# Order tables, a DRAM stop for attention outputs and one work list for a two-layer encoder's token sublayer

## The chip, the core and the metric

The kernel runs on one core of a Trainium2 chip. The core has five engines that run side by side and wait for each other through semaphores: TensorE (PE; its weight loads, PEld, overlap its matmuls), VectorE (DVE), ScalarE (ACT), GpSimd (POOL) and SyncE (SP). Data lies in DRAM, in SBUF (128 partitions) and in PSUM, which PE writes. DMAs are issued from SP's queue and from POOL's and share 16 DMA engines. The metric is the device time of one execution in microseconds; shorter is better.

## What is computed

A two-layer bidirectional encoder on one sequence of 512 tokens, width 1024, in float32. Cut to what matters:

```python
for i in range(DEPTH):                                   # DEPTH = 2
    proj = x @ w_in[i]                                   # 1024 -> 6656 columns
    q_na, k_na, v_na, q_r, k_r, v_r, g_r, gate_a, gate_b = jnp.split(proj, IN_SPLITS, axis=-1)
    ya = neighbourhood_attention(q_na, k_na, v_na, na_rpb[i])            # 8 heads of 64
    yb = bidirectional_retention(q_r, k_r, v_r, g_r, ...)                # 4 heads, 128 | 256
    merged = jax.nn.sigmoid(gate_a) * (ya @ w_branch_a[i]) + jax.nn.sigmoid(gate_b) * (yb @ w_branch_b[i])
    y = merged @ w_out[i]
    x = layer_norm(DEEPNORM_ALPHA * x + y, ln1_g[i], ln1_b[i])
    ffn = conv_glu_ffn(x, w_up[i], conv_w[i], conv_b[i], w_down[i])
    ple = jax.nn.sigmoid(x @ w_ple_gate[i]) * (p[i] @ w_ple_proj[i])
    x = layer_norm(DEEPNORM_ALPHA * x + ffn + ple, ln2_g[i], ln2_b[i])
```

## The kernel before

**Products.** Every operand of a matmul is split into two parts, `hi` (the value rounded to the matmul's input format) and `lo` (the rest), by a copy on ACT and a subtraction on DVE (`split`, lines 207 and 208). A product is three matmuls, hi by hi, hi by lo and lo by hi (`mm3`, lines 537 to 539). Weights come from DRAM as `raw` tiles of 128x1024 by SP's queue and are split on chip; of some tiles (`sent`) ACT makes both parts and POOL's queue adds the weight into `lo` by an accumulating DMA (line 495).

**Blocks.** The two value/retention-gate blocks (0 and 1) and the two gate blocks (2 and 3) of the input projection, the branch b product (B) and others are multiplied as a two by two block scheme with seven products instead of eight, `a, c, t1, t2, d, t3, t4`. Their operands are sums of quarters of weights and of activations. A sum of weights is made either by an accumulating DMA on POOL's queue (line 433) or, where a table (`ON_CHIP`, `BB_CHIP`) says so, by an addition on DVE (line 474). The sums of activations come from `quad_sums` (DVE at lines 916 to 931, parts at 909 and 912). A finished quarter of a block's result goes to an `emit`: gates pass through a sigmoid on ACT and are stored to DRAM (`gscr`), value blocks are split and kept.

**Space.** SBUF holds 30 `unit` tiles of 4 KB per partition (`N_UNIT`); split activations, intermediate results, loaded gates and some weights all take one and give it back after its last reader. A DMA into a unit waits until the earlier owner's readers are done, and everything behind it on the same queue waits too.

**Order.** In the token sublayer a head of the list, `VG[l]`, and then the list `FILL[l]` of each layer say which product comes next: `3t2` is product t2 of block 3, `nq1` and `nk1` are attention query and key projections, `q0` and `k0` those of retention, `vn` the attention values, `b` a quarter of branch a (`ba`: two token tiles by 512 columns), `Ba` to `Bt4` branch b's products, `P` one token tile of the output projection. Between the entries stand steps of the retention heads (`ret_head`, from the slots in `RET_AT` with offsets 0, 2, 3, 5) and the attention heads (`na_head`, from `NA_AT` with offsets 0, 2, 5). From the end of `VG` to the end of the sublayer the work is put in its final order by a scheduler from the order in which the code issues it; elsewhere the code's order is kept.

**The end of the sublayer.** `ya` are the attention outputs; turned and split they lie in four units `yat` (one per pair of heads) until branch a reads them. `ba` loads the four gate tiles `sa` of a token tile each and multiplies branch a into them (line 1282). `branch_b` is a generator: at its products it also loads the second gate (`M`, line 1306), makes the split quarters of `Y`, the retention output, and their sums (`yw`, `yq`), and after each product but the first it transposes (`turn`, line 1267, tile `tr`) what the product before it finished; behind the last product it transposes the last pairs. The turned result `mt` is the operand of the output projection (`proj_ln`, tile `gn`).

`early_x` (lines 1247 and 1252) multiplies and adds the normalisation's parameters into the residual `R` at the start of layer 1, at the slots of `PX_AT`. `PG[l]` is the order of the block behind the token sublayer (the per-layer embedding's gate together with the first up-projection tiles, `up`).

Of the kernel before, what the change touches and what calls it, by code (L numbers as in the profile page):

```python
# [14 lines left out]
P = 128  # L15
# [17 lines left out]
SENT = (('k0', 'nk2', 'q0', 'q2', 'q3', 'q1'), ('nq1', 'q3', 'nq3', 'k0'))  # L33
# [4 lines left out]
FILL = (('nk0', 'nq3', '3t2', '3d', 'vn', 'nq2', '3t3', 'nk2', '2c', '3t4', '2t1', '0a', '2d', '2t2',  # L38
# [7 lines left out]
RET_AT = ((36, 37, 38, 40), (38, 40, 38, 41))  # L46
NA_AT = ((8, 10, 13, 14, 15, 20, 21, 24), (8, 8, 9, 11, 14, 18, 19, 24))
ORD = ('vector', 'scalar', 'tensor', 'gpsimd', 'sync')
RESIDENT = {(l, c) for l in range(DEPTH) for c in (67, 68, 69, 70, 71)}
TURN_LAG = 1  # L50
OUT_PREP = ((0, 1, 2, 1), (0, 1, 1, 1))
# [3 lines left out]
VG = (('p0', 'p1', '3a', '3c', 'nq1', 'nk1', '2a', 'nq0', 'nk3', '3t1'),  # L55
      ('3a', '3c', '2a', 'nk2', '3t1', 'nq0', 'nq2'))

XN_AT = (0, 6)
M_AT = (1, 1)
TABLES_AT = (0, 8)  # L60
REST_AT = (1, 2, 5, 8, 11, 16)
SUM_AT = (-2, -1)
PLE_AT = (45, 22)
HOOK = (1, 1)
PX_AT = (8, 15, 15, 18, 19, 22, 39, 42, 42, 42)
GN_ACT = ((0, 1, 2, 3), (3,))
BSENT = (('4d', '1d'), ('4d',))
# [3 lines left out]
PG = (('a', 'c', 't1', 'up', 'up', 't2', 'Ua', 'Ut1', 'd', 't3', 'Ut2', 'Ud', 't4', 'Ut3', 'Uc', 'Ut4'),  # L71
 ('a', 'c', 't1', 'up', 'up', 't2', 'Ua', 'Ut1', 'd', 't3', 'Ut2', 'Ud', 't4', 'Ut3', 'Uc', 'Ut4'))
# [4 lines left out]
BB_CHIP = ('t2', 't2')  # L77
# [8 lines left out]
 ('D0a', 'D0c', 'D2c', 'U0c', 'u12', 'u13', 'u14', 'u2', 'u3', 'u5', 'u6', 'u9'))  # L86
# [26 lines left out]
ON_CHIP = (('t2 t3', 't2', '', ''), ('', '', 't1 t3', 't2 t3'))  # L113
BB_HELD = (('c', 'd', 't2', 't4', 't1'), ('c', 't2', 't4'))
BB_EARLY = ('a', 'd')
RC_ACT = ((0, 5), (4, 7))


def _ap(t, off, dims):
# [2125 lines left out]
```

## Time and profile before

| | us |
|---|---|
| three timed runs | 1665.73, 1665.70, 1664.40 (median 1665.7) |
| the profiled execution | 1665.84 |
| its span, first to last instruction | 1664.1 |
| DMA moved | 326.79 MB, mean 196 GB/s |
| busy: PE, DVE, ACT, POOL | 1642.6, 1350.8, 1049.6, 226.7 |

In rows of the profile a line number is that of the kernel; `out<-in` are the program's names without their numbers; `x` counts instructions. A busy PE is modelled: a matmul's row of 0.39 us begins 0.23 us after the row before it where nothing waits. In the timeline a bracket behind a row says how long the engine was idle before it and who ended that. "u", "v" and "w" are accumulators of the block products, "gt" of a projection by columns, "gn" of one by tokens.

The page's slices of the span (40 slices of 41.6 us, busy tenths) show PE at nine everywhere but in the last:

```profile
PE   9999999999999999999999999999999999999997
DVE  5857878878787988978988766789888889889788
ACT  6787875665367757447586887753644676564563
POOL 1101111111211210111100011100202211101112
```

### The profile page before, as it was taken

To read this page: it belongs to the slowest core of one execution; us is meant where nothing else is said; L and a number is where in the kernel's file an instruction comes from. 1 tells how busy PE (TensorE), PEld (TensorE's weight loads), DVE (VectorE), ACT (ScalarE), POOL (GpSimd) and SP (SyncE) were. 2 spreads that over 40 slices of the span, in tenths; PEclk is the share of its full clock that TensorE was granted. 3 is DMA by queue.
4 is the path that set the end of the run, shared out by engine and by line. 5 is a ranking of instruction groups with operands and counts; after the bars stand their busy time and mean duration, and the time that the engine had idled before them with its cause. 6 is when DMAs were issued, how large, how long until landed. Compare 5 with 4: busy or idle time off the path is not lost.

```text
span 1664.1 us, 23407 instructions
## 1 busy us (share of the span) xinstructions
PE 1642.6 (99%) x8679; PEld 1407.9 (85%) x8679; DVE 1350.8 (81%) x2063; ACT 1049.6 (63%) x1586; POOL 226.7 (14%) x277
## 2 busy tenths in 40 slices
PE   9999999999999999999999999999999999999997
PEld 7888888987889899889888888888878898988896
DVE  5857878878787988978988766789888889889788
ACT  6787875665367757447586887753644676564563
POOL 1101111111211210111100011100202211101112
PEclk9999999999999999999999999999999999999999
DMA  9859865566789877479656579533758897875693
GB/s 329 237 154 215 239 143 132 177 210 161 210 228 246 209 228 228 138 206 226 201 170 199 165 177 249 118 102 114 208 183 256 220 270 178 253 203 176 180 239 76
DMA packets 95442, 326.79 MB, mean 196 GB/s; under 512 B 10976, under 2 KB 11488, under 8 KB 95328
## 3 DMA queue, kind: packets, MB, share of 16 engines
q0 software_dynamic: 33984, 121.65, 36.3%
q1 hardware_dynamic: 61200, 203.39, 34.6%
q8 instruction: 68, 1.11, 0.3%
q14 instruction: 46, 0.38, 0.1%
q10 hardware_dynamic: 144, 0.26, 0.0%
HBM read 300.09 MB, written 26.21 MB: 196 GB/s over the span
## 4 chain that ended last, share of the span: by engine, by line
PE 87%; DVE 6%; issue 2%; DMA 2%; ACT 2%; POOL 0%; DVEq 0%; POOLq 0%; ACTq 0%
PE u L537 7%; PE u L539 7%; PE u L538 7%; PE gt L537 6%; PE u L138 6%; PE gt L539 6%; PE gt L538 6%; PE v L537 4%; PE v L539 4%; PE v L538 4%; PE gt L138 4%; PE v L138 4%; PE gn L537 3%; PE gn L538 3%; PE gn L539 3%
## 5 line engine op out<-in xcount | busy, mean ns | idle before, releaser
L208 DVE TENSOR_TENSOR lo<-rawa,hi 128x1024 fp32r<-128x1024 f32 (+1 forms) x150 | 178.6, 1201 | 58.6 <-ACT hi L207 57.9
L207 ACT CAST hi<-rawa 128x1024 fp32r<-128x1024 f32 (+1 forms) x150 | 153.4, 1034 | 102.0 <-DMA rawa<-in_wpack 30.3
L208 DVE TENSOR_TENSOR lo<-raw,hi 128x1024 fp32r<-128x1024 f32 x109 | 132.4, 1222 | 38.6 <-ACT hi L207 38.4
L433 POOL DMA_DIRECT2D rawa<-in_wpack x84 | 75.1, 894 | 556.9 <-DVE lo L208 427.1
L207 ACT CAST hi<-raw 128x1024 fp32r<-128x1024 f32 x109 | 113.4, 1049 | 58.2 <-DMA raw<-in_wpack 14.1
L537 PE MATMUL gt<-x1t,hi 128*128 128x512 f32 x256 | 100.2, 391 | 1.8 <-DVE ca L1568 1.8
L538 PE MATMUL gt<-x1t,hi 128*128 128x512 f32 x256 | 99.8, 390 | 0.0
L539 PE MATMUL gt<-x1t,lo 128*128 128x512 f32 x256 | 99.3, 389 | 0.0
L537 PE MATMUL gt<-xt,hi 128*128 128x512 f32 x224 | 87.7, 392 | 0.0
L539 PE MATMUL gt<-xt,lo 128*128 128x512 f32 x224 | 87.3, 390 | 0.0
L538 PE MATMUL gt<-xt,hi 128*128 128x512 f32 x224 | 87.3, 390 | 0.0
L495 POOL DMA_DIRECT2D lo<-in_wpack x34 | 30.3, 890 | 382.0 <-ACT lo L494 264.5
L138 DVE TENSOR_TENSOR lo<-rawa,hi 128x1024 fp32r<-128x1024 f32 x38 | 45.7, 1222 | 17.6 <-ACT hi L138 17.6
L537 PEld LDWEIGHTS gt<-x1t,hi 128*128 128x128 f32 x256 | 48.1, 188 | 12.9 <-issue 2.6
L539 PEld LDWEIGHTS gt<-x1t,lo 128*128 128x128 f32 x256 | 48.1, 188 | 10.1
L538 PEld LDWEIGHTS gt<-x1t,hi 128*128 128x128 f32 x256 | 48.1, 188 | 9.4
L207 ACT CAST hi<-rawt 128x1024 fp32r<-128x1024 f32 (+1 forms) x38 | 38.7, 1027 | 23.8 <-DVE rawt L474 14.3
L208 DVE TENSOR_TENSOR lo<-rawt,hi 128x1024 fp32r<-128x1024 f32 (+1 forms) x38 | 45.0, 1196 | 7.2 <-ACT hi L207 3.9
L138 ACT CAST hi<-rawa 128x1024 fp32r<-128x1024 f32 (+1 forms) x42 | 42.5, 1028 | 12.8 <-DMA rawa<-in_wpack 5.2
L537 PE MATMUL gn<-hi,mt 128*128 128x512 f32 x128 | 50.2, 395 | 0.0
L537 PE MATMUL u<-hi,s 128*128 128x512 f32 x128 | 50.0, 392 | 0.0
L538 PE MATMUL u<-lo,s 128*128 128x512 f32 x128 | 49.9, 390 | 0.0
(523 smaller groups left out, 5551.2 us busy)
## 6 DMA issues: line engine op xcount, KB each, us to landing
raw<-in_wpack SPq DMA_DIRECT2D x173, 512.0 KB, 5.2
rawa<-in_wpack POOLq DMA_DIRECT2D x108, 512.0 KB, 6.4
rawa<-in_wpack SPq DMA_DIRECT2D x46, 512.0 KB, 5.5
rawt<-in_wpack SPq DMA_DIRECT2D x46, 512.0 KB, 6.0
lo<-in_wpack POOLq DMA_DIRECT2D x44, 512.0 KB, 7.7
s<-s_scr POOLq DMA_DIRECT2D x32, 512.0 KB, 8.9
rawd<-in_wpack SPq DMA_DIRECT2D x30, 512.0 KB, 6.3
rawt<-in_wpack POOLq DMA_DIRECT2D x26, 512.0 KB, 8.2
```

The source lines that it names most:

```text
L138: r = f(*a, **k)
L207: nc.scalar.copy(hi, src)
L208: nc.vector.tensor_sub(lo, src, _f(hi))
L433: nc.gpsimd.dma_start(it.raw[:, :w], wpack[l, c][:, o:o + w], accum_op=ALU.add)
L495: nc.gpsimd.dma_start(lo[:, :w], wpack[l, c][:, o:o + w], accum_op=ALU.add)
L537: nc.tensor.matmul(ps, lh, rh, start=start, stop=False, skip_group_check=more)
L538: nc.tensor.matmul(ps, lh, rl, start=False, stop=False, skip_group_check=more)
L539: nc.tensor.matmul(ps, ll, rh, start=False, stop=stop, skip_group_check=more)
```

## The change

**Attention outputs wait in DRAM.** Of the four `yat` units of a layer, three (`Y_KEPT`) are stored to a new DRAM tensor `yscr` by SP's queue when they are made, and are loaded again by POOL's queue at the list entry `Y`.

**Branch b is split into list entries.** What `branch_b` did around its products has entries of its own in `FILL`: `Q` makes the next split quarter or sum (seven of them: a, c, t1, t2, d, t3, t4), `A` loads the next quarter of the first gate, `M` of the second, `X` loads the residual, `T` does two turns. These entries take no slot of their own.

**Gates by quarter.** `sa` and `M` were four tiles each of one token tile by 1024 columns; now they are four of two token tiles by 512, loaded one at a time, and a tile is given back after its second turn or use. The bytes are the same.

**The transposes of a retention head** come in two steps, one per pair of token tiles, with offsets of their own; retention and attention heads get offsets per head (`RET_OFF`, `NA_OFF`).

**New numbers** in most of the order tables: `FILL`, `VG`, the slots, which weights are `sent`, held or added on chip. By engine, counting rows of the built programs: PE 8692 and 8692; DVE 2065 and 2068, among them additions `rawt<-rawt,rawd` 20 and 26, scalings of `yb` 12 and 8; ACT scalings of `yb` 20 and 24, table loads 39 and 37; POOL accumulating loads `rawt<-in_wpack` 26 and 20, `yat<-y_scr` 0 and 6; SP stores `y_scr<-yat` 0 and 6.

The core of the diff:

```diff
-         '1d', 'q0', '1t2', 'q1', '0c', 'q2', '1t3', 'q3', '1t4', 'b', 'b', 'b', 'b', 'Ba', 'Bc',
-         'Bt1', 'Bd', 'Bt2', 'Bt3', 'Bt4'),
-        ('nk0', 'nq1', '3d', '3t2', 'nk1', '2c', '3t3', '3t4', 'vn', '2t1', '2d', '2t2', 'nk3', '0a',
...
-         'k1', 'k2', '1t3', '1d', '0c', 'q0', '1t4', 'q1', 'k3', 'q3', 'b', 'b', 'b', 'b', 'Ba',
-         'Bc', 'Bt1', 'Bd', 'Bt2', 'Bt3', 'P', 'Bt4', 'P'))
...
+         'k3', 'k1', '1d', 'q0', '1t2', 'q2', '1c', 'Y', '1t3', 'q3', '1t4', 'A', 'A', 'A', 'A', 'b',
+         'M', 'b', 'b', 'Q', 'Ba', 'Q', 'X', 'b', 'Q', 'Bc', 'Q', 'Bt1', 'Q', 'M', 'Q', 'Q', 'Bt2',
+         'Bd', 'M', 'Bt3', 'M', 'Bt4', 'T', 'T', 'T', 'P', 'T'),
...
+         'Y', 'k0', '0t4', '1t2', 'k2', '1t3', 'A', '0c', 'k1', 'q1', '1t4', 'k3', 'A', 'A', 'b',
+         'M', 'b', 'A', 'b', 'Q', 'Ba', 'b', 'Q', 'Q', 'Bt1', 'Bc', 'M', 'Q', 'M', 'Q', 'Q', 'M',
+         'Q', 'Bd', 'Bt2', 'X', 'Bt3', 'T', 'T', 'Bt4', 'T', 'P', 'T'))
...
+Y_KEPT = ((0, 1, 2), (0, 1, 3))
...
-PX_AT = (8, 15, 15, 18, 19, 22, 39, 42, 42, 42)
+PX_AT = (8, 14, 17, 18, 20, 24, 39, 42, 42, 42)
...
-BB_CHIP = ('t2', 't2')
+BB_CHIP = ('t1 t3', 't2')
...
-ON_CHIP = (('t2 t3', 't2', '', ''), ('', '', 't1 t3', 't2 t3'))
+ON_CHIP = (('t2 t3', 't1 t2 t3', '', 't3'), ('', 't3', 't2 t3', ''))
...
+                    if m in Y_KEPT[l]:
+                        stores.append((yscr[m], _f(u.rearrange("p s c -> p (s c)"))))
+                        del yat[m]
...
+            def gate_load(g, z, name, hb, tp):
+                z[hb, tp] = unit_f(name, (P, 2, 512))
+                nc.sync.dma_start(z[hb, tp], gscr[g][tp * 256:(tp + 1) * 256, hb * 512:(hb + 1) * 512].rearrange("(t p) c -> p t c", p=P))
...
+            def ya_load():
+
+                for m in Y_KEPT[l]:
+                    yat[m] = unit_r("yat")
+                    nc.gpsimd.dma_start(yat[m].rearrange("p s c -> p (s c)"), yscr[m])
...
+                def prep():
+                    for kind, q, h in (("a", 0, 0), ("c", 1, 0)):
+                        quad(kind, q, h)
+                        yield
+                    for _ in range(4):
+                        next(sums)
+                        yield
+                    quad("t4", 1, 1)
+                    yield
...
+                def turn2():
+                    for _ in range(2):
+                        turn(*turns.pop(0))
...
-                    due = len(turns)
-                    step(kind)
-                    for _ in range(due if TURN_LAG else len(turns)):
-                        turn(*turns.pop(0))
-                    n += 1
```

Where it moves instructions, first on PE at the end of branch b in layer 0. Before, behind the last product (t4, accumulator `u`), stand the turns of the gated quarters `sa` and then the first projection step:

```order
L538 MATMUL u_3495<-lo_3757,yq_3750 128x512
L539 MATMUL u_3495<-hi_3756,yq_3751 128x512
L1267 MATMUL tr_3889<-ident,sa_3164 128x128 x4
L1267 MATMUL tr_3898<-ident,sa_3166 128x128 x4
L1267 MATMUL tr_3905<-ident,sa_3164 128x128 x4
L1267 MATMUL tr_3914<-ident,sa_3166 128x128 x4
L537 MATMUL gn_3936<-hi_3774,mt_3683 128x512
```

In the change there are three turns behind that product, of quarters finished by earlier products, and then the projection:

```order
L545 MATMUL u_3463<-lo_3750,yq_3702 128x512
L546 MATMUL u_3463<-hi_3749,yq_3703 128x512
L1294 MATMUL tr_3891<-ident,sa_3151 128x128 x4
L1294 MATMUL tr_3898<-ident,sa_3153 128x128 x4
L1294 MATMUL tr_3907<-ident,sa_3153 128x128 x4
L544 MATMUL gn_3924<-hi_3767,mt_3871 128x512
```

and the pair that the last product feeds (`sa_3149`) comes behind the whole first token tile of the projection:

```order
L545 MATMUL gn_3924<-lo_3919,mt_3887 128x512
L546 MATMUL gn_3924<-hi_3918,mt_3888 128x512
L1294 MATMUL tr_3955<-ident,sa_3149 128x128 x4
L1294 MATMUL tr_3964<-ident,sa_3149 128x128 x4
L544 MATMUL gn_3972<-hi_3767,mt_3871 128x512
```

The last pair of turns has moved by one token tile of the projection, 24 matmuls. Second, on DVE in layer 0, between branch b's products a and t1. Before, `yw<-s` are the low parts of t1's operand (`s_655` its first half, `s_656` its second), `p<-p,w` adds product c's accumulator to product a's:

```order
L912 TENSOR_TENSOR yw_3477<-s_655_3580,yw_3477 128x512
L474 TENSOR_TENSOR rawa_2871<-rawa_2871,rawd_3339 128x1024
L474 TENSOR_TENSOR rawa_3000<-rawa_3000,rawd_3512 128x1024
L208 TENSOR_TENSOR yw_3477<-Y_3559,yw_3477 128x512
L916 TENSOR_TENSOR s_656_3582<-Y_3559,Y_3304 128x512
L921 SCALAR_TENSOR_TENSOR s_663_3631<-s_655_3580,Y_3196 128x512
L835 TENSOR_TENSOR p_648_3555<-p_648_3555,w_3588 128x512
L912 TENSOR_TENSOR yw_3477<-s_656_3582,yw_3477 128x512
L835 TENSOR_TENSOR p_649_3556<-p_649_3556,w_3589 128x512
```

In the change the halves are `s_653` and `s_654`:

```order
L924 TENSOR_TENSOR s_654_3580<-Y_3450,Y_3196 128x512
L214 TENSOR_TENSOR lo_3495<-raw_3476,hi_3494 128x1024
L1314 TENSOR_TENSOR sa_3153<-gn_3564,sa_3153 128x512
L920 TENSOR_TENSOR yw_3457<-s_653_3578,yw_3457 128x512
L920 TENSOR_TENSOR yw_3457<-s_654_3580,yw_3457 128x512
L214 TENSOR_TENSOR lo_3589<-rawa_2838,hi_3588 128x1024
L929 SCALAR_TENSOR_TENSOR s_663_3633<-s_653_3578,Y_3183 128x512
L214 TENSOR_TENSOR lo_3606<-rawa_3115,hi_3605 128x1024
L844 TENSOR_TENSOR p_643_3522<-p_643_3522,w_3586 128x512
```

Both low parts now stand ahead of the additions of product c, and the two weight additions have gone from here. Third, on PE in the block behind the token sublayer of layer 1: before, product t1 (`v`, on the sums `s`) follows product c (`w`):

```order
L138 MATMUL w_12140<-hi_12051,x1t_11739 128x512 x2
L138 MATMUL w_12140<-lo_12052,x1t_11739 128x512
L138 MATMUL w_12140<-hi_12051,x1t_11739 128x512
L138 MATMUL v_12191<-hi_12055,s_12131 128x512
L138 MATMUL v_12191<-lo_12056,s_12131 128x512
```

In the change an up-projection tile (`gt`) follows it:

```order
L144 MATMUL w_12144<-hi_12071,x1t_11730 128x512 x2
L144 MATMUL w_12144<-lo_12072,x1t_11730 128x512
L144 MATMUL w_12144<-hi_12071,x1t_11730 128x512
L144 MATMUL gt_12213<-x1t_11730,hi_12075 128x512 x2
L144 MATMUL gt_12213<-x1t_11730,lo_12076 128x512
```

Product t1 has moved behind two such tiles, 48 matmuls.

More of the change, by code (lines that the diff above doesn't have):

```diff
@@ L299, in vg_items @@
                     continue
-                out += by[k] if k in by else plain_items(l, k)
+                if k not in "QMTXYA":
+                    out += by[k] if k in by else plain_items(l, k)
             return out if "P" in seen else out + by["P"]
@@ L659, in trunk @@
         _Ordered.on = set(ORD)
-        ws.late = {2: [], 3: []}
+        ws.late = {int(k[0]): [] for k in VG[0] if k[1:] == "a"}
         hd = [unit_f("hd") for _ in range(2)]
@@ L1102, in ret_head @@
                 Y[q, kp] = unit_f("Y", (P, 2, 2, 256))
-                for dv in range(2):
+                for i in range(2):
+                    if i:
+                        yield
                     ps = bank("ybt")
-                    for t in range(4):
-                        nc.tensor.transpose(ps[:, t * P:(t + 1) * P], yb[:, t, dv * P:(dv + 1) * P], ident)
-                    nc.scalar.copy(Y[q, kp][:, dv].rearrange("p a b -> p (a b)"), ps)
+                    for dv in range(2):
+                        for t in range(2):
+                            nc.tensor.transpose(ps[:, (2 * dv + t) * P:(2 * dv + t + 1) * P], yb[:, 2 * i + t, dv * P:(dv + 1) * P], ident)
+                    nc.scalar.copy(Y[q, kp][:, :, i, :], ps.rearrange("p (a b) -> p a b", a=2))
+                    YH[q, i, kp] = Y[q, kp][:, :, i, :]
                 yield
@@ L1480, in fillers @@
                     if f[0] == "B":
-                        if bbs is None:
-                            send()
-                            bbs = branch_b()
-                            next(bbs)
-                        bbs.send(f[1:])
+                        bb["step"](f[1:])
                         yield
@@ L1507, in fillers @@
                     yield
-                bbs.send(None)
+                assert not bb["turns"]
             fl = fillers()
```

138 lines of the change are left out of this document (70 added, 68 removed), and 5 rows, old and new, of the table FILL.

## Prediction

> **What bounds the kernel now.** I read the page first, then the stretches of the span, then the list of what TensorE (PE) waited for, then those waits one by one in the timeline.
>
> ```profile
> span 1664.1 us, 23407 instructions
> PE 1642.6 (99%) x8679; PEld 1407.9 (85%) x8679; DVE 1350.8 (81%) x2063; ACT 1049.6 (63%) x1586; POOL 226.7 (14%) x277
> ```
>
> PE is busy for all but 1664.1 - 1642.6 = 21.5 us. The profiled execution took 1665.84 us, 1.7 more than its span; the median of the three timed runs is 1665.7. I count against 1665.84, and the two stand 0.1 us apart. The change neither adds nor removes a matmul or a transpose: the order lists 8692 PE rows for both kernels. So it can win no more than idle time of PE that lies where its orders reach. The stretches (PE, PEld, DVE, ACT, POOL busy us, granted clock, DMA share, GB/s) show how little that is:
>
> ```profile
> 0.00:450.00 450.00, 446.62 (x2204) 373.33 (x2205) 341.62 (x582) 302.62 (x496) 54.00 (x66) 1.00 0.72 200
> 450.00:850.00 400.00, 397.48 (x2241) 348.22 (x2240) 339.74 (x465) 248.46 (x342) 61.94 (x79) 1.00 0.77 214
> 880.00:925.00 45.00, 43.77 (x201) 36.37 (x201) 40.30 (x51) 30.91 (x46) 1.73 (x2) 1.00 0.60 183
> 1170.00:1250.00 80.00, 77.18 (x377) 63.60 (x376) 66.25 (x101) 41.77 (x59) 9.07 (x11) 1.00 0.69 200
> 1600.00:1665.00 65.00, 54.37 (x259) 45.21 (x257) 59.02 (x96) 28.67 (x39) 14.72 (x14) 0.93 0.55 122
> ```
>
> The last row is the tail, about ten of the 21.5 us (the span ends at 1664.1), which no edit touches. The token sublayer of layer 0 (up to about 430) loses 3.4 us, that of layer 1 most at 880 to 925 and at 1170 to 1250: 1.2 and 2.8. Who ended those waits (total us, times, longest):
>
> ```profile
> PE gt L537 <- DVE ca L1568: 1.8, 2, 1.0
> PE tr L1267 <- DVE sa L1312: 1.6, 3, 0.7
> PE v L537 <- ACT yw L909: 1.3, 1, 1.3
> PE v L138 <- DMA lo<-in_wpack: 1.3, 1, 1.3
> PE u L537 <- DVE p L856: 1.2, 1, 1.2
> PE warm L646 <- DVE warm L643: 1.2, 1, 1.2
> PE v L138 <- ACT s L138: 0.8, 1, 0.8
> PE v L539 <- DVE yw L912: 0.5, 1, 0.5
> PE u L539 <- DVE yw L912: 0.5, 1, 0.5
> PE tr L1267 <- issue: 0.3, 1, 0.3
> PE u L538 <- DVE lo L208: 0.3, 1, 0.3
> PE w L539 <- DVE k L208: 0.2, 1, 0.2
> PE o L537 <- ACT su L207: 0.2, 1, 0.2
> ```
>
> `tr` are the turns, `yw` the operands of branch b, `p` a gate or value block, `su` the retention state: ten waits of the token sublayers, 1.6 + 1.3 + 1.2 + 0.5 + 0.5 + 0.3 + 0.3 + 0.2 = 5.9 us. `v L138 <- ACT s` is the block behind the token sublayer of layer 1, whose order PG changes as well: 0.8. The rest (`ca`, `lo<-in_wpack`, `k`) is the channel sublayer, the same work in both kernels.
>
> A wait costs more than its idle time:
>
> ```profile
> 921.93 0.50 PE L537 MATMUL u<-hi,xt 128*128 128x512 f32 x1 [1.23 <-DVE p L856]
> 922.27 0.39 PE L538 MATMUL u<-lo,xt 128*128 128x512 f32 x1
> 922.49 0.40 PE L539 MATMUL u<-hi,xt 128*128 128x512 f32 x1
> 922.73 0.39 PE L537 MATMUL u<-hi,xt 128*128 128x512 f32 x1
> ```
>
> Matmuls that take 0.39 start 0.23 apart, so they overlap by 0.16. After a wait that overlap is gone, and the next start comes 0.34 later, not 0.23: another 0.11. A wait costs its idle time and 0.27 us. Eleven waits: 5.9 + 0.8 + 11 x 0.27 = **9.7 us, the most that the change can win**, which would give 1656.1.
>
> **The turns.** Now a block product's turns stand right behind the next product, and the last two pairs right behind the last product; PE waits for the vector chain (gate product, sum) that feeds them.
>
> ```profile
> 368.27 0.50 PE L539 MATMUL v<-hi,yw 128*128 128x512 f32 x1 [0.54 <-DVE yw L912]
> 402.57 1.26 PE L1267 MATMUL tr<-ident,sa 128*128 128x128 f32 x8 [0.51 <-DVE sa L1312]
> 1194.79 0.50 PE L537 MATMUL v<-hi,yw 128*128 128x512 f32 x1 [1.32 <-ACT yw L909]
> 1290.03 0.50 PE L138 MATMUL v<-hi,s 128*128 128x512 f32 x1 [0.84 <-ACT s L138]
> ```
>
> The wait at 402.57 is the last pair. In the changed order a whole projection step, 24 matmuls by 0.227 = 5.4 us, stands between the last product and that pair, and the earlier pairs come two or more products after their sums. The chain they wait for is four DVE operations of 0.69 (two gate products, two sums), 2.8 us. All four waits of `tr` go: 1.6 + 0.3 + 4 x 0.27 = 3.0. What would be late next is the projection's operand `mt` of the last turn, with two ready token tiles ahead of it.
>
> **The operands of branch b.** At 368.27 PE has begun t1 and waits for its second half. In DVE's order that half (`yw<-s`) stands behind `p<-p,w`, which itself waits for the product before. The change puts both halves, and t2's first step, ahead of `p<-p,w`. The two `DVE yw` waits of layer 0 go: 1.0 + 2 x 0.27 = 1.5. In layer 1 (1194.79, 1.3 idle) ACT's copy came late, behind a cast that waited for a weight's DMA; there the changed order puts t1 ahead of c, so its operand is also wanted earlier. Nothing here shows that it is in time: bounds 0 and 1.6 us, I take half, 0.8.
>
> **The block behind it and the start of layer 1.** PG of layer 1 now has one up tile pair, two products of 24 matmuls (10.9 us), ahead of t1. That covers 0.84 of waiting for the copy of `s` many times: 0.8 + 0.27 = 1.1 won. At 921.93 DVE was behind: 40.30 us busy in the 45 us from 880. The new order moves blocks 2 and 3 forward and spaces the multiplications of the residual differently (PX_AT), with the same number of operations. Bounds 0 and 1.5; I take 1.0, since a backlog of 1.2 us is small and the products there are all in other places. The waits on `lo` and `su` I leave as they are.
>
> Gains: 3.0 + 1.5 + 0.8 + 1.1 + 1.0 = **7.4 us**.
>
> **What is added.** Three attention tiles per layer are stored (SP's queue) and loaded again (POOL's queue), six 512 KB stores and six such loads in all, 6.3 MB, while the DMA share up to 450 us is 0.72. The gate loads are the same bytes in quarters. By the order, DVE gets six more additions `rawt<-rawt,rawd`, net, in place of six accumulating loads on POOL, and loses four scalings of `yb` to ACT.
>
> ```profile
> L474 DVE TENSOR_TENSOR rawt<-rawt,rawd 128x1024 f32<-128x1024 f32 x20 | 24.3, 1222 | 7.9 <-DMA rawd<-in_wpack 6.1 <-DMA rawt<-in_wpack 1.8
> L1099 DVE TENSOR_SCALAR yb<-yb,rstd 128x256 f32<-128x256 f32 x12 | 3.8, 350 | 2.3 <-POOL rstd L587 2.3
> ```
>
> That is 6 x 1.22 - 4 x 0.35 = +5.9 us of DVE; layer 0 alone gets eight of the additions more, six of them behind 200 us, or 7.3 us. Is there room?
>
> ```profile
> 220.00:270.00 50.00, 50.00 (x234) 41.82 (x233) 36.30 (x52) 35.49 (x51) 6.96 (x8) 1.00 0.69 164
> 270.00:320.00 50.00, 50.00 (x293) 44.27 (x292) 47.59 (x89) 35.30 (x63) 3.19 (x4) 1.00 0.34 104
> 320.00:360.00 40.00, 40.00 (x241) 35.45 (x240) 27.42 (x67) 19.02 (x35) 6.93 (x9) 1.00 0.70 226
> 360.00:400.00 40.00, 38.52 (x177) 30.42 (x176) 39.68 (x55) 27.85 (x39) 4.32 (x5) 1.00 0.67 158
> ```
>
> DVE does 151.0 us in these 180; 13.7 us are free at 220 to 270 and 12.6 at 320 to 360, and by the order the new additions stand in just these two stretches, and two old ones leave the full stretch from 360. So I price them at nothing; without that cover they cost their 7.3 us. The loads have two deadlines.
>
> ```profile
> raw<-in_wpack SPq DMA_DIRECT2D x173, 512.0 KB, 5.2
> lo<-in_wpack POOLq DMA_DIRECT2D x44, 512.0 KB, 7.7
> rawt<-in_wpack POOLq DMA_DIRECT2D x26, 512.0 KB, 8.2
> M<-g_scr SPq DMA_DIRECT2D x8, 512.0 KB, 6.4
> ```
>
> The third y load of layer 0 waits for a unit that a retention product frees; PE has 15.9 us of work (by the counts of its rows and their spacing) before branch a reads it, and the load needs 0.9 to issue and about 8.2 to land. Behind it on POOL stand the `rstd` powers of the retention heads, which the group norm waits for; the unit is freed before those heads' products end, so they lose about a microsecond that the scores behind them cover. In layer 1 the loads come 70 us ahead. The third gate quarter of layer 0 can be issued only when the d product has read its weights, and must have landed (6.4) when the t3 product, 5.4 us behind, is gated: late by 1 us on DVE, with turns 5 us behind it. I can't see how DVE's tighter order meets all of this: between no new wait and three like the longest of the list (3 x (1.3 + 0.27) = 4.7), I take 2.4, half.
>
> **Sum**: 1665.8 - 7.4 + 2.4 = **1660.8 us**.
>
> **Weighed against the trace.** POOL's DMAs land here in 6.4 to 8.2 us beside a DVE busy for 81% of the span. The Trainium skill (SBUF — State Buffer, "SBUF: two separate sides" and the section on the bandwidth pool behind it) speaks against loads on this queue: a DMA issued from GpSimd cannot write its descriptors while DVE holds the port pair that the two share, and one such DMA took about 3100 ns for 620. By that rule the traces' landings should be several times those of SP's queue, where raw weights land in 5.2; they are about half as long again (7.7 and 8.2), so it hardly shows here. What it would do in this kernel is the fourth rival.
>
> **Rivals.** *The waits only change place.* DVE has 40 of 40 us to do from 360, and what is done earlier fills 270 to 360; each wait taken away leaves DVE as late for the next product. For it: the 0.5 us waits of `yw` and `sa` all end on DVE. Against: PE loses nothing at 270 to 320 although DVE is at 95%. It keeps the 3.0 of the turns and 1.1 of PG and has new waits of 2.4: about 1664. Chance 0.27.
> *All goes, nothing new*: 9.7 won, about 1656.5. Against it: layer 1's t1 ahead of c. Chance 0.12.
> *DVE becomes the bound of layer 0* (slower): the additions wait for `rawd` DMAs (6.1 us of such idle in their row), DVE's queue is in order, and what stands behind them is late from 346 on. If they cost 7.3 us and idle at the row's rate for ten more (10 x 0.4 = 4), and the layer's gains (about 3) are lost, then 1665.8 - 4.4 + 2.4 + 7.3 + 4 = about 1675; it decides when DVE's work from 320 to 400 passes the 80 us of PE there, now 67.1. Chance 0.09.
> *The y loads are late*: if each of the three issues took five times its 0.9, the third would start about 5 us later and land about 8 later than counted, against a slack of some 7 (15.9 us of PE work less 9.1): PE waits about 1 us in layer 0, and the time is 1662. That is the mechanism of the skill's rule above. Chance 0.02.
>
> **How the numbers follow.** Forecast 0.50, of which 0.46 lie below 1662.4, 0.2% under the median, about what a measurement of this kernel can tell from no change. Faster 0.46 + 0.12 = 0.58; the second case counts as same but for 0.02 that end over 1669.0, so same 0.04 + 0.25 + 0.02 (late loads) = 0.31; slower 0.09 + 0.02 = 0.11. The range: from 1656.5, nearly the most that can be won, to 1666.5, where the bounds of the unknown waits and most of the second case are in and the slower one is left out. The likeliest case alone has 1658 to 1663.
>
> **What would show it.** Right: no PE wait on `tr` in layer 0 and none on `yw` there; the PG wait gone; idle of PE from 0 to 430 under 2 us. Wrong: PE waits on `DVE lo` or `yw` between 340 and 400, DVE busy through 320 to 400 without a gap (the rivals); PE's first `gn<-yat` ended by a DMA; or the channel sublayer, whose waits of 1 us come and go with its DMAs, different by more than 2 us, which I did not count.

## The result, and the profile after

The kernel after the change took 1654.9 us (median of 6 runs, 1654.3 to 1657.3), the kernel before 1664.1 beside it (6 runs, 1662.5 to 1665.7): a ratio of 0.9946 with a 95% interval of 0.9933 to 0.9959, 9 us less. In a second series the same two files gave 1656.2 (5 runs) against 1664.1 (18 runs), 0.9956 [0.9944, 0.9968], 7.3 us less by the ratio and 7.9 by the medians. The forecast was 1660.8, 5.0 less than the profiled execution of before; the sign was right, the gain was larger.

The page of the kernel after, first its span, then the busy time of each engine with its share of the span and its instructions:

```profile
span 1652.8 us, 23446 instructions
PE 1639.8 (99%) x8679; PEld 1409.9 (85%) x8679; DVE 1355.9 (82%) x2066; ACT 1046.9 (63%) x1587; POOL 224.2 (14%) x276
```

PE's idle time went from 21.5 to 13.0 us. DVE got 5.1 us more to do, as forecast (5.9), and ACT and POOL a little less. What PE waited for in this kernel (line, then total us, times, longest) is now a list of four:

```profile
PE warm L653 <- DVE warm L650: 1.2, 1, 1.2
PE ns L1194 <- DVE kl L1156: 1.1, 1, 1.1
PE ybt L1117 <- ACT yb L1105: 0.7, 1, 0.7
PE gt L544 <- DVE ca L1597: 0.3, 1, 0.3
```

`warm` is the start of the program, in both kernels, and `ca` the channel sublayer. All eleven waits that the prediction counted (the `tr`, `yw`, `p`, `lo` and `su` rows, and the one on `s`) are gone. Two are new, both in layer 1: the neighbourhood scores wait for `kl`, the transposes of a retention head for `yb`. Their places in the timeline of PE (start, duration, engine, line, in brackets the idle time ahead):

```profile
920.94 0.39 PE L1194 MATMUL ns<-kl,qn 128*128 128x256 f32 x1 [1.05 <-DVE kl L1156]
...
1185.32 0.95 PE L1117 MATMUL ybt<-ident,yb 128*128 128x128 f32 x4 [0.66 <-ACT yb L1105]
```

The stretches of this kernel (length, then busy PE, PEld, DVE, ACT, POOL, granted clock, DMA share, GB/s):

```profile
0.00:450.00 450.00, 448.53 (x2216) 377.00 (x2217) 352.40 (x591) 305.19 (x504) 49.12 (x61) 1.00 0.68 199
450.00:850.00 400.00, 399.61 (x2253) 350.52 (x2252) 336.94 (x461) 249.04 (x341) 63.86 (x83) 1.00 0.79 216
880.00:925.00 45.00, 43.95 (x201) 36.57 (x201) 35.78 (x48) 28.38 (x46) 0.00 (x0) 1.00 0.63 228
1170.00:1250.00 80.00, 79.28 (x386) 66.05 (x385) 63.93 (x95) 41.72 (x57) 11.12 (x13) 1.00 0.78 237
```

The reader sees four things. Up to 450 us PE idles 1.5 us instead of 3.4, and that includes the 1.2 of `warm`. From 880 to 925 nothing was won (43.95 against 43.77): the wait on `kl` has taken the place of the one on `p`, although DVE has 4.5 us less to do there. From 1170 to 1250 the idle time went from 2.8 to 0.7. And the stretch from 450 to 850, the same code in both kernels, went from 397.48 to 399.61: 2 us of the difference between these two traces lie where nothing was edited. That is the last of the signs by which the prediction said that it would be wrong (2.1 us, where it named 2); the repeated traces below take it up.

DVE's load from 360 to 400 us is easily misread from the shares alone:

```profile
360.00:400.00 40.00, 39.88 (x189) 33.00 (x187) 39.15 (x56) 25.95 (x37) 5.28 (x6) 1.00 0.81 204
```

DVE is as full as before (39.15 of 40, before 39.68), yet PE loses 0.1 us instead of 1.5. DVE's load alone did not make the waits; what differs is the order of the work, on DVE and on PE. That is read from the two traces; no run below tests it in this place.

### The profile page after: what moved, and what is told of

The parts are those of the page before. It is cut to its first block, busy times and chain, and to the rows that moved or that the text cites. A ratio compares the mean times of both kernels' runs of the same rounds, so it can differ in the third digit from the quotient of the medians.

```text
span 1652.8 us, 23446 instructions
## 1 busy us (share of the span) xinstructions
PE 1639.8 (99%) x8679; PEld 1409.9 (85%) x8679; DVE 1355.9 (82%) x2066; ACT 1046.9 (63%) x1587; POOL 224.2 (14%) x276
## 4 chain that ended last, share of the span: by engine, by line
PE 93%; DVE 3%; DMA 3%; issue 0%; ACT 0%; DVEq 0%; SPq 0%; POOL 0%; ACTq 0%; POOLq 0%
PE u L544 7%; PE u L546 7%; PE u L545 7%; PE u L144 7%; PE gt L544 6%; PE gt L546 6%; PE gt L545 6%; PE v L144 4%; PE v L544 4%; PE v L545 4%; PE v L546 4%; PE gt L144 4%; PE gn L544 4%; PE gn L546 4%; PE gn L545 4%; PE w L546 2%
## 5 line engine op out<-in xcount | busy, mean ns | idle before, releaser
L213 ACT CAST hi<-rawa 128x1024 fp32r<-128x1024 f32 (+1 forms) x150 | 153.6, 1033 | 113.0 <-DMA rawa<-in_wpack 31.1
L214 DVE TENSOR_TENSOR lo<-raw,hi 128x1024 fp32r<-128x1024 f32 x105 | 127.6, 1220 | 29.2 <-ACT hi L213 25.2
L213 ACT CAST hi<-raw 128x1024 fp32r<-128x1024 f32 x105 | 109.6, 1051 | 57.5 <-DMA raw<-in_wpack 12.3
L545 PE MATMUL gt<-x1t,hi 128*128 128x512 f32 x256 | 99.8, 390 | 0.0
L545 PE MATMUL gt<-xt,hi 128*128 128x512 f32 x224 | 87.2, 389 | 0.0
L544 PEld LDWEIGHTS gt<-x1t,hi 128*128 128x128 f32 x256 | 48.1, 188 | 11.1 <-ACT hi L213 0.9
L545 PEld LDWEIGHTS gt<-x1t,hi 128*128 128x128 f32 x256 | 48.1, 188 | 9.4
L544 PE MATMUL u<-hi,s 128*128 128x512 f32 x128 | 50.2, 393 | 0.0
L545 PE MATMUL u<-lo,s 128*128 128x512 f32 x128 | 49.9, 390 | 0.0
L546 PE MATMUL u<-hi,s 128*128 128x512 f32 x128 | 49.9, 390 | 0.0
```

The costliest lines, as they stand in the source:

```text
L213: nc.scalar.copy(hi, src)
L214: nc.vector.tensor_sub(lo, src, _f(hi))
L544: nc.tensor.matmul(ps, lh, rh, start=start, stop=False, skip_group_check=more)
L545: nc.tensor.matmul(ps, lh, rl, start=False, stop=False, skip_group_check=more)
L546: nc.tensor.matmul(ps, ll, rh, start=False, stop=stop, skip_group_check=more)
```

## The experiments

Theory A: the gain is the waits in the edited places, all of them, less the two new ones; what else differs between two traces comes and goes. Rivals are named with each run. Each kernel was timed in five rounds beside the kernel before, whose median was between 1664.1 and 1664.2 in every series.

**Both kernels again**, with no edit.

> The kernel before, unchanged, profiled a second time. In the two profiles at hand the change gained 2.8 us in the token sublayer of layer 0, 2.9 in that of layer 1, but also 2.7 between the end of the first and the last turn of layer 0's channel sublayer (449 to 848 us) and 2.6 behind layer 1's token sublayer, where only the block behind it was edited. Theory A (the edited waits alone): PE's waits on tr, yw and p and the one on s recur, about 6.7 us idle in sum; the waits of the channel sublayer (on lo of a weight, on ca) come and go, so that its stretch from 450 to 850 is shorter or longer than in the first profile by 1 us or more. Theory B (the change acts on the channel sublayer too): the same waits on lo and ca stand in this profile as well, PE busy within 0.5 us of 397.5 in 450 to 850. Median 1663 to 1665 by both.

> The kernel after, unchanged, profiled a second time. Theory A: the two waits left in layer 1's token sublayer (ns on kl, 1.1; ybt on yb, 0.7) recur, and the channel sublayer shows waits of its own in other places, 1 to 4 us in sum, as before's did. Theory B: PE is busy for at least 399 of the 400 us from 450 to 850 again. Median 1654 to 1656, ratio 0.993 to 0.996 by both.

Measured: 1663.9 and 1656.2. The second trace of before, PE's waits without `warm`:

```profile
PE tr L1267 <- DVE sa L1312: 1.5, 3, 0.7
PE v L537 <- ACT yw L909: 1.5, 1, 1.5
...
PE v L138 <- ACT s L138: 0.8, 1, 0.8
...
PE u L537 <- DVE p L856: 0.6, 1, 0.6
PE gt L539 <- DVE lo L138: 0.6, 1, 0.6
PE v L539 <- DVE yw L912: 0.5, 1, 0.5
PE u L539 <- DVE yw L912: 0.5, 1, 0.5
PE u L538 <- DVE lo L208: 0.3, 1, 0.3
...
PE tr L1267 <- issue: 0.3, 1, 0.3
...
PE o L537 <- ACT su L207: 0.2, 1, 0.2
```

The waits that the prediction counted are the same ones within 0.2 us, except that on `p`, which is half as long. Those of the channel sublayer are not: the 1.3 us on a weight's `lo` (at 544 us) is gone, and so is one of the two on `ca`. Two waits stand where the first trace has none, 0.6 at the start (`gt L539 <- DVE lo`, at 67 us) and 0.3 on a weight's load in layer 1's token sublayer (at 886 us, left out above). In the second trace of after the list is that of the first, with 0.5 on `yb` and two rows of 0.2 to 0.3 more. The stretch of the channel sublayer in the second traces of before and of after, one row of each:

```profile
450.00:850.00 400.00, 399.00 (x2253) 349.90 (x2252) 341.11 (x467) 249.08 (x343) 61.93 (x79) 1.00 0.78 215
```

```profile
450.00:850.00 400.00, 399.39 (x2250) 349.94 (x2249) 336.50 (x461) 248.49 (x341) 63.55 (x82) 1.00 0.80 215
```

The 2 us have become 0.4. So they belong to one execution of before, not to the change, and theory B (the change acts on the channel sublayer too) has lost most of its ground; the next run takes the rest. The expectation had after's own channel waits at 1 to 4 us; they are under 1.

**The block behind layer 1 alone**, in the kernel before:

```diff
-  ('a', 'c', 't1', 'up', 'up', 't2', 'Ua', ...
+  ('a', 'c', 'up', 't1', 'up', 't2', 'Ua', ...
```

> The kernel before with one edit of the change: the block behind layer 1's token sublayer takes one up tile pair ahead of t1. Theory A: PE's wait of 0.8 us on s near 1290 us goes and nothing takes its place: 1.1 us, about 1663.0 beside a before of 1664.1, a ratio of 0.9993. Rival (it only changes place): the same time, with a wait of about 0.8 on another operand of that block. The trace of this run also samples the channel sublayers of before a third time: Theory A has PE busy 397 to 399.6 us of the 400 from 450 to 850, different from run to run; Theory B (the change acts there) has it below 399.1 in every run of before's orders.

Measured: 1662.8 against 1664.2, 0.9991 [0.9982, 1.0000]. The time alone would not carry it; the trace does: the wait on `s` is gone and no row behind t1 has taken its place (a new one of 0.2, on `xn` at 1262.5 us, stands ahead of the block's edited part). And this third trace of before's orders has PE busy for 399.43 of the 400 us from 450 to 850:

```profile
450.00:850.00 400.00, 399.43 (x2256) 350.45 (x2254) 340.68 (x467) 250.22 (x344) 61.86 (x79) 1.00 0.78 216
```

The kernels with after's orders have 398.8 to 400.0 there in all their traces: theory B falls.

**Turns nearer to their sums**, in after:

```diff
-         'Bd', 'M', 'Bt3', 'M', 'Bt4', 'T', 'T', 'T', 'P', 'T'),
+         'Bd', 'M', 'Bt3', 'T', 'M', 'Bt4', 'T', 'T', 'T', 'P'),
...
-         'Q', 'Bd', 'Bt2', 'X', 'Bt3', 'T', 'T', 'Bt4', 'T', 'P', 'T'))
+         'Q', 'Bd', 'Bt2', 'X', 'Bt3', 'T', 'T', 'Bt4', 'T', 'T', 'P'))
```

> The kernel after with the turns of branch b nearer to their sums: in layer 0 the first pair one product earlier and the last pair ahead of the projection's first step instead of behind it, in layer 1 the last pair ahead of the projection's last step. Theory A (distance from sum to turn is what took the waits of tr away): PE waits on sa again at the last pair of each layer, 0.5 to 0.9 idle each and 0.27 more, 1.5 to 2.5 us in sum, 1656 to 1657. Rival (the sums come earlier, so the distance is no longer needed): no wait on tr, the time of after within 0.5 us.

Measured: 1658.3, 0.9967 [0.9955, 0.9978], 2.0 us above the repeated after. Only the last pair has moved in the trace: ahead of the last product three turns stand in both kernels. PE's timeline in layer 0 behind the last product, first the three turns that were there, then the last pair; and DVE's sums:

```profile
398.19 1.47 PE L1294 MATMUL tr<-ident,sa 128*128 128x128 f32 x12
...
399.79 1.27 PE L1294 MATMUL tr<-ident,sa 128*128 128x128 f32 x8
400.82 0.48 PE L544 MATMUL gn<-hi,mt 128*128 128x512 f32 x1
```

```profile
399.00 1.28 DVE L1349 TENSOR_TENSOR sa<-sa,M 128x512 f32<-128x512 f32 x2
```

Theory A holds in layer 0, though the list of waits shows next to nothing there (an idle time of 0.12 ahead of the last pair). The pair starts 1.8 us behind the start of the last product's last matmul (397.97 to 399.79), just as before (400.79 to 402.57): the sums come no earlier. Before, 8 transposes stood in that time, here 12, which cover 0.4 us more of it. Where nothing waits, a group of 12 takes 1.23 us to the next matmul (in after, at 398.70) and one of 8 takes 0.79 (in before, at 1220.83), so a transpose takes 0.11; by that 20 would take 2.1, and here they take 2.63: 0.5 us are lost, of the 0.9 that the 16 of before lose in the same way (401.02 to 403.58). In layer 1 the last pair, put ahead of the last projection step, waits 2.0 us, more than it ever did before (0.7); PE's row, and DVE's ahead of it:

```profile
1224.20 1.27 PE L1294 MATMUL tr<-ident,sa 128*128 128x128 f32 x8 [2.04 <-issue]
```

```profile
1219.95 2.35 DVE L214 TENSOR_TENSOR lo<-raw,hi 128x1024 fp32r<-128x1024 f32 x2
...
1223.41 1.28 DVE L1349 TENSOR_TENSOR sa<-sa,M 128x512 f32<-128x512 f32 x2
```

The trace names no releaser ("issue"), but the first of the two sums ends 0.1 us ahead of the transposes that read it. Before that, DVE makes two remainders of weights while the last product ends (at 1221.3), so the new order needs the distance here more than the old one did.

**The sums later**, in after: `Q`, a step that prepares an operand of branch b, put back a product or two in the lists of both layers; in layer 1 this puts product c ahead of t1 again.

```diff
-  'Q', 'Ba', 'Q', 'X', 'b', 'Q', 'Bc', 'Q', 'Bt1', 'Q', 'M', 'Q', 'Q', 'Bt2',
+  'Q', 'Ba', 'X', 'b', 'Q', 'Q', 'Bc', 'Q', 'Bt1', 'M', 'Q', 'Bt2', 'Q', 'Q',
...
-  'Q', 'Q', 'Bt1', 'Bc', 'M', 'Q', 'M', 'Q', 'Q', 'M', 'Q', 'Bd', 'Bt2', 'X', 'Bt3', ...
+  'Q', 'Q', 'Bc', 'Q', 'Bt1', 'M', 'M', 'Q', 'Bd', 'M', 'Q', 'Q', 'Bt2', 'X', 'Bt3', ...
```

> The kernel after with the steps that prepare branch b's operands put back to the places of before (each a product or two later, layers 0 and 1). Theory A: the two or three waits on yw return, 1.0 idle in layer 0 and up to 1.3 in layer 1, with 0.27 each: 1.5 to 3.1 us, 1656.5 to 1658. Rival (DVE has been relieved in these stretches by work moved elsewhere, so that the places do not matter): under 0.5 us, no wait on yw.

Measured: 1660.2, 0.9974 [0.9963, 0.9985], 3.9 us above the repeated after. Two waits of PE are new, and neither is on `yw`:

```profile
PE u L544 <- ACT hi L213: 2.9, 1, 2.9
PE v L545 <- DMA lo<-in_wpack: 1.6, 1, 1.6
```

The 2.9 stand in layer 1 at 1203.7 us: a product waits for the cast `hi` of its own weight. ACT's cast ahead of it, first in this kernel, then in the repeated after:

```profile
1201.65 1.99 ACT L213 CAST hi<-rawa 128x1024 fp32r<-128x1024 f32 x2 [3.67 <-DMA rawa<-in_wpack]
```

```profile
1199.48 1.05 ACT L213 CAST hi<-rawa 128x1024 fp32r<-128x1024 f32 x1 [1.93 <-DMA rawa<-in_wpack]
```

ACT stands 3.7 us for a weight's load here and 1.9 in after, and the product behind it waits in turn. With c and t1 exchanged their weights are in another order too, so the run shows that the place is worth some 3 us in layer 1, but not how much of it is the sums. The 1.6 us on `lo` in layer 0 (at 384.5 us) cannot be laid to the edit: it stood at 0.3 in the repeated after, at the same place, and at 1.8 in a later run whose layer 0 is unedited (below). In layer 0 this run does not test the place of t1's operands at all: the scheduler has left them where they were, 4.1 us ahead of `p<-p,w` (at 369.24 here, at 370.02 in after). DVE in this kernel, then in after:

```profile
365.17 1.28 DVE L920 TENSOR_TENSOR yw<-s,yw 128x512 fp32r<-128x512 f32 x2
```

```profile
365.95 1.28 DVE L920 TENSOR_TENSOR yw<-s,yw 128x512 fp32r<-128x512 f32 x2
```

Only the steps for d, t3 and t4 have moved there, so that no wait on `yw` came back in layer 0 says nothing. What took those two waits away is read from the traces alone (below).

**No stop in DRAM**, in after: the turned attention outputs stay in SBUF, six stores and six loads of 512 KB go.

```diff
-Y_KEPT = ((0, 1, 2), (0, 1, 3))
+Y_KEPT = ((), ())
```

> The kernel after without the stop in DRAM: the turned attention outputs stay in SBUF in both layers, so six stores and six loads of 512 KB go and six buffers stay taken some 70 to 200 us longer. Theory A (the waits went through the order, the stop only frees buffers): weights come later, but no wait appears that costs over 1 us: 1656 to 1657. Rival (the stop is what lets weights come in time): PE waits on DMA (raw, lo, rawt) between 100 and 430 or 900 and 1170, 3 us or more in sum, 1659 and up.

Measured: 1665.5, 1.0012 [1.0003, 1.0021]: slower than the kernel before, 9.3 us above the repeated after. The rival is right in the time. PE's two longest rows, both new, and one of the places on ACT behind which they stand, a weight's cast that a product of PE releases late:

```profile
PE s L544 <- ACT qk L213: 3.6, 2, 2.3
PE u L545 <- DVE lo L214: 1.9, 2, 1.4
```

```profile
259.81 1.05 ACT L213 CAST hi<-raw 128x1024 fp32r<-128x1024 f32 x1 [4.39 <-PE gt L545]
```

```profile
0.00:450.00 450.00, 441.47 (x2162) 368.06 (x2163) 343.31 (x576) 299.05 (x489) 44.52 (x56) 1.00 0.65 185
```

PE idles 8.5 us up to 450 in this kernel (the row above; after 1.5), and not on DMA rows, as the rival had it, but on casts and remainders. I read the releaser on ACT (`PE gt`) as a buffer that a product still held; in after's list of PE no such wait is left. So, by this reading, the buffers that the stop frees let layer 0's weights be cast in time; the time is shown by the run, the way to it is argued. Where it is needed:

```diff
-Y_KEPT = ((0, 1, 2), (0, 1, 3))
+Y_KEPT = ((0, 1, 2), ())
```

> The kernel after with the stop in DRAM in layer 0 only. Without it in both layers the kernel took 1665.5 us, and its trace has the loss between 270 and 330 us, in layer 0, while its layer 1 was no slower. Theory A (the stop pays in layer 0, where weights are short of buffers, and earns nothing in layer 1): the time of after within 1 us, 1655 to 1657. Rival (layer 1's order needs it too, and only the slack of a layer that starts late hid it): 2 us or more slower, with PE waits on s or u between 1040 and 1170.

Measured: 1657.5, 0.9960 [0.9947, 0.9972], against 0.9956 [0.9944, 0.9968] of the repeated after: not told apart. Beside the known wait on `kl`, layer 1 has none on `s` or `u`, only one of 0.3 on `gt` at 1073 us. Of the 9.3 us that the stop is worth, 8 lie in layer 0.

**Sums of weight tiles back on the DMA**, in after:

```diff
-BB_CHIP = ('t1 t3', 't2')
+BB_CHIP = ('t2', 't2')
...
-ON_CHIP = (('t2 t3', 't1 t2 t3', '', 't3'), ('', 't3', 't2 t3', ''))
+ON_CHIP = (('t2 t3', 't2', '', ''), ('', '', 't1 t3', 't2 t3'))
```

> The kernel after with the sums of weight tiles left as before (eight additions of 1.22 us in layer 0's token sublayer go back from DVE to accumulating loads on POOL's queue). Theory A (DVE's additions were covered, cost nothing): within 0.7 us of after, 1655.5 to 1657. Rival 1 (they cost DVE time that shows): 1 to 3 us faster. Rival 2 (the accumulating loads are what comes late, and putting them on DVE is a gain of the change): PE waits on DMA lo or on casts behind it, 1 us or more, 1657.5 and up.

Measured: 1683.4, 1.0115 [1.0101, 1.0129], 27 us above the repeated after. Theory A is wrong by far in what the additions are worth, if not in what they cost. PE's two longest waits, and the cast behind the second of them, which waits 10 us for a weight:

```profile
PE v L544 <- DVE vl L214: 5.6, 1, 5.6
PE gt L144 <- ACT hi L144: 4.2, 1, 4.2
```

```profile
44.58 1.04 ACT L144 CAST hi<-raw 128x1024 fp32r<-128x1024 f32 x1 [10.48 <-DMA raw<-in_wpack]
```

Up to 450 us PE idles 21.4 us. An accumulating load waits on POOL's queue until its base has landed, in after for 19.0 us in three of them up to there, here for 36.3 in four, and what stands behind it on that queue waits too. That PE's waits come from there is argued; no row leads from the one to the other. The kernel before lives with this same table, in its own order of blocks and holds; the new order does not. In layer 1 the old table also has one sum more on DVE. So this run prices the pair "new order, old sums", not the additions by themselves. Their cost on DVE has its own run.

**More work for DVE**, in after: behind eight of layer 0's additions the sum is multiplied by one in place.

```diff
                         nc.vector.tensor_add(it.raw[:, :it.width], it.raw[:, :it.width], o.raw[:, :it.width])
+                        self.nadd = getattr(self, "nadd", 0) + 1
+                        if 8 < self.nadd <= 16:
+                            nc.vector.tensor_scalar_mul(it.raw[:, :it.width], it.raw[:, :it.width], 1.0)
```

> The kernel after with DVE burdened on purpose: behind each of eight weight-tile additions in layer 0's token sublayer (about 170 to 360 us) the sum is multiplied by one in place, 8 more operations of 128x1024, about 1.2 us each by the additions' own duration, 9.8 us of DVE (the additions that the change brought were counted as 7.3). Theory A (DVE has room there, additions are covered): within 1 us of after, 1655.5 to 1657. Rival (DVE is the bound of layer 0): 4 to 10 us slower, PE waits on DVE lo and on casts behind it between 180 and 400.

Measured: 1657.3, 0.9960 [0.9947, 0.9972]: 1.1 us above the repeated after, where theory A had 1 at most, its intervals one over the other. The burden was smaller than meant: the operation took 0.69 us, not 1.2, so 5.5 us in all, where the change's own additions were counted as 7.3. From 180 to 400 us PE was busy for 219.67 of 220:

```profile
180.00:400.00 220.00, 219.67 (x1147) 187.45 (x1146) 197.88 (x335) 143.59 (x240) 19.46 (x25) 1.00 0.57 164
```

After has 219.85 there, and PE's list has no wait on a weight's `lo`. The eight stand at 231 to 242 and at 351 to 383 us, beside the additions themselves; DVE had that room in those places.

**The wait on `kl`**, in after, layer 1's first list:

```diff
-        ('3t2', '2c', '3d', 'nq1', '3t3', 'nk1', 'nk0', '3t4', 'vn', ...
+        ('3t2', '2c', '3d', 'nq1', '3t3', 'nk0', 'nk1', '3t4', 'vn', ...
```

> The kernel after with the keys' first two groups of layer 1 in the other order (nk0 ahead of nk1), so that 11 us of products and not 5.4 stand between nk0 and the first scores that read its remainder kl. Theory A (the wait on kl at 921 is the price of the new order at the start of layer 1, in place of the one on p): that wait goes, 1.05 idle and 0.27: 1.3 us faster than after, 1653.5 to 1655. Rival (DVE and ACT are behind there whatever the order): a wait of 0.6 to 1.2 on another operand between 915 and 925, the time of after.

Measured: 1655.5, 0.9944 [0.9931, 0.9956]. The wait on `kl` is gone, and 0.6 us stands three matmuls further in the same scores, on another operand:

```profile
922.45 0.39 PE L1193 MATMUL ns<-kn,qn 128*128 128x256 f32 x1 [0.62 <-ACT sg L887]
```

Theory A and its rival share this one. In time it is not told apart from after. Two additions to it, one with the last head's output product a slot earlier, one with the stop in layer 0 only:

```diff
-           ((0, 2, 4, 5, 7), (0, 1, 3, 4, 4), (0, 2, 3, 5, 7), (0, 1, 4, 5, 5)))
+           ((0, 2, 4, 5, 7), (0, 1, 3, 4, 4), (0, 2, 3, 5, 7), (0, 1, 3, 5, 5)))
```

> The kernel with nk0 ahead of nk1 and, beside it, the last retention head's output product of layer 1 one slot earlier, which gives its scaling on ACT 5 to 6 us more before the turns ybt read it. Theory A (the wait of 0.5 to 0.7 on yb at 1185 us is a distance too short): no wait on yb, up to 0.9 us faster than e10, 1654 to 1655. Rival (the product one slot earlier waits for its state su): a wait on su or o of the same size near 1170, the time of e10.

> nk0 ahead of nk1 and the stop in DRAM in layer 0 only. If both theories of e10 and e13 hold: 1653.5 to 1655.5, the wait on kl gone and no new wait in layer 1; if the stop of layer 1 pays, 2 us or more slower than e10.

Measured: 1656.7, 0.9958 [0.9945, 0.9970], and 1656.1, 0.9957 [0.9944, 0.9971]. In the first, other waits came in layer 1 (1.0 on `yq`, 0.4 on `hi`), and one of 1.8 in layer 0, which the edit does not touch: nothing won. That the wait on `yb` is gone says nothing for the edit: nk0 ahead of nk1 alone has none either, nor have *turns nearer* and *more work for DVE*, which leave that place as it is. The second is as expected but for 0.3 on a weight's remainder at 1069 us, which the kernel with the stop in layer 0 only has too; it has neither of after's two waits, and its profiled execution, 1654.1, is among the fastest of all; its median is after's. No version beats the change by what these rounds can tell.

## Why the prediction was right in its sign and short in its size

- **What bounds the kernel, and the ceiling of 9.7 us.** Right as a list: the eleven waits were what the change could reach, and it reached all eleven. On the second pair of traces, the waits that the prediction counted are 6.2 us of idle time in before and the two new ones 1.6 in after; nine waits fewer at 0.27 are 2.4, so 4.6 + 2.4 = 7.0, and the waits elsewhere in the two lists give about another 1.3. That is 8.3, and the spans differ by 9.0; in the first pair the same count gives 11.1 for 11.3. So the price of a restart, 0.27, held, where the clock did not fall (last section).
- **Turns, 3.0.** Right in amount and reason: the four waits are gone, and without the distance the last pair is late again, by 2.0 us of idle time in layer 1 and by 0.5 in all in layer 0.
- **Operands of branch b.** Layer 0, 1.5: both waits gone, but the first was misread. What PE waits for at 368.27 is the low part of the *first* half of t1's operand, which stands on DVE behind remainders of weights, not behind `p<-p,w`:

```profile
366.39 1.22 DVE L208 TENSOR_TENSOR lo<-rawa,hi 128x1024 fp32r<-128x1024 f32 x1
367.53 0.68 DVE L912 TENSOR_TENSOR yw<-s,yw 128x512 fp32r<-128x512 f32 x1
...
372.37 0.69 DVE L835 TENSOR_TENSOR p<-p,w 128x512 f32<-128x512 f32 x1
```

  In after both halves are done at 367.2 and PE, which now does the whole of c first, begins t1 only at 369.7. Which of the two moves takes the wait away is not shown. Layer 1, half of 1.6: all of it went.
- **The block behind, 1.1.** Right, and shown alone: its wait went and none replaced it.
- **The start of layer 1, 1.0 of 1.5.** Wrong: the place won next to nothing. The wait on `p` went, and 1.05 us on `kl` came: nk0 had moved to stand 24 matmuls ahead of its reader. In the account below it is counted as gone here and as new there.
- **The waits on `lo` and `su`, left as they are.** Wrong: they went as well, 0.3 + 0.2 + 2 x 0.27 = 1.0.
- **New waits, 2.4.** Right in size by luck: (1.05 + 0.27) + (0.66 + 0.27) = 2.3. The 2.4 was reckoned for the loads and gate quarters of layer 0, where after's two traces have next to none; the two that came are in layer 1, and that on `yb` is in only some of the traces. One place in layer 0 has become tight that was not reckoned with: a weight's load (`v L545 <- DMA lo`, at 383 us) is late by 0.1 and 0.3 us in the two traces of after and by 1.6 and 1.8 in two of the edited kernels; no trace of before's orders has a wait there.
- **DVE's additions at nothing.** Right: 5.5 us more of the kind cost no more than could be measured, and *DVE the bound of layer 0* falls. That they could not be left out of this order was not seen.
- **The stop in DRAM at nothing, with a risk from late loads.** The cost is right. The loads of layer 0 take 0.5 to 0.6 us each to issue, from 300.1 to 305.1 us, and land 3.6 us later; branch a first reads `yat` at 320.2:

```profile
yat<-y_scr POOLq DMA_DIRECT2D x3, 512.0 KB, 3.6
```

  That is half of what the weights' loads on that queue took in before (7.7 and 8.2), with DVE busy for 82% of the span, so the fourth rival falls. The rule of the Trainium skill (SBUF — State Buffer) that spoke for it, whose measured case is a copy on DVE, does not show in this kernel, where DVE mostly adds and subtracts tiles. What the stop gives, buffers for layer 0's weights worth 9 us in the new order by the run without it, was missing from the sum; it is not a gain over before, but what holds the other gains.

**The step that failed is the sum of the gains, "7.4 us".** Three of its terms were set too low for want of proof: the operands of layer 1 by 0.8, the start of layer 1 by 0.5, `lo` and `su` by 1.0. The rows of those waits are missing in both traces of after, so the three terms measured 1.6, 1.5 and 1.0 where the sum had 0.8, 1.0 and nothing (by the waits; none of the three was timed by itself, and at the start of layer 1 the wait on `kl` took 1.3 back). The edited places won 9.7 - 2.3 = 7.4 net, where the forecast had 7.4 - 2.4 = 5.0. That is 2.4 of the 5.9 us by which the first series came out under the forecast. Another 1.7 are the start of the count: 1665.84 lies above all six runs of before in the first series, and the median of before in all four series is 1664.1 to 1664.2. I took a median of three for the level and read from it that the profiled execution was typical. The last 1.8 (0.5 in the second series) I lay to waits outside the edited places, which come and go by 1 to 2 us from run to run; that is not shown by a run, and the two series of after differ by 1.3 themselves. The range had its lower end at the ceiling counted from that same high start, so it could not hold a full success: from 1664.1 the same ceiling would have been 1654.4.

*The waits only change place*, the strongest rival, is true of one place, the start of layer 1.

## What to carry to other kernels

An engine that is busy for 39 of 40 us tells little about whether another waits for it; whether its next result is the one that is wanted does, so read the order of the queue beside its load. Where a change takes aim at every wait in a list, either take each at its full price and put the doubt into the term for new waits, or halve them and leave that term out; doing both counts the doubt twice. Count from a median of several runs, not from the one execution that has a trace, and take a second trace of an unchanged kernel before reading a difference of 2 us in a stage that nobody edited. Tables that were fitted together (holds, sums, order) can't be priced by putting one of them back.

## What the runs showed of the hardware that was not expected

A wait of PE can cost far more than its idle time and a restart. In the run with the output product a slot earlier, PE waited 1.82 us for a weight; the matmuls ran on at 0.39 each, and 1.5 us later they slowed down to 0.63 (PE's timeline, then the stretch):

```profile
384.97 0.50 PE L545 MATMUL v<-lo,yq 128*128 128x512 f32 x1 [1.82 <-DMA lo<-in_wpack]
...
386.48 0.63 PE L545 MATMUL v<-lo,yq 128*128 128x512 f32 x1
...
389.87 0.39 PE L544 MATMUL u<-hi,yq 128*128 128x512 f32 x1
```

```profile
385.00:390.00 5.00, 5.00 (x15) 4.00 (x16) 4.22 (x6) 1.87 (x2) 0.86 (x1) 0.66 0.82 209
```

From 386.48 to 389.87 us, 3.4 us, eight matmuls started 0.42 apart, the granted clock of the stretch being 0.66: 1.6 us more on a wait of 1.8. Waits of 2.0 and 2.9 us in other runs here (at 1224.2 and 1203.7) were not followed by it, while one of 2.3 in the run without the stop was (at 328.2: three matmuls of 0.63, granted clock 0.50 from 329.0 to 330.8), so a wait of this length may or may not bring it on. Besides the start of the program, no trace of these runs has 128x512 matmuls slowed like this but behind waits of over 1.5 us. The Trainium skill (TensorE: Matmul & The Clock Gate, Part 1) has the array at half clock after an idle window of about 3.4 us and until one busy window of that length has passed; the length of the slow stretch agrees, but here less than 2 us of idle time was enough.
